# Delta rule's decay matrices: one exponential per head behind a subtraction by VectorE, and the keys' norm factor by a root, multiplied in afterwards

## The chip, the cores and the metric

One core of a Trainium2 chip runs the whole kernel. The metric is the device time of one execution in microseconds, the median of several runs. Times of single instructions come from one profiled execution.

## The reference

One block on 1024 tokens of width 1024, all in float32: a modulated RMS norm, one projection `h @ w_in`, two mixers side by side (dilated attention with 8 heads, and a gated delta rule with 8 heads), `w_out`, then a gated feed-forward and a final norm. The change lies in the delta rule alone. Cut to it:

```python
qkv = silu(causal_conv(concat([q, k, v]), conv_w))      # width 4, per channel
q = l2norm(q) * HEAD_DIM ** -0.5                         # per head of 64
k = l2norm(k)                                            # k * rsqrt(sum(k*k) + EPS)
gcum = cumsum(g)                                         # per chunk and head
diff = gcum[..., :, None] - gcum[..., None, :]
decay = where(causal, exp(where(causal, diff, 0)), 0)
a_mat = where(strict, einsum('cd,ed->ce', k_beta, k) * decay, 0)
sol = triangular_solve(a_mat + I, concat([v * beta, k_beta * exp(gcum)]))
qk = where(causal, einsum('cd,ed->ce', q, k) * decay, 0)
# then a scan over the chunks: v_new, o_i, state
```

## The kernel before

The program runs through these stages: modulation and norm, the projections of `w_in`, the delta rule in two groups `g` of four heads, attention, `w_out`, the feed-forward and the final norm. Each float32 product of the projections is three matmuls over operands split in a high and a low part (names `wh_`, `wl_`, `hh`, `hl`; 512 columns each at L590, 256 at L613). ScalarE makes the high part of a weight, GpSimd the low part (L231).

The delta rule takes chunks of 128 tokens, so a group has 8 chunks `n` for each of its 4 heads. Two heads lie side by side in one tile of 128 partitions. For a group:

1. **Convolutions** (`conv`): ScalarE scales the input into the target, VectorE adds three shifted terms (L553), ScalarE applies SiLU (L557). For group 0 this stands in `delta`, for group 1 in `delta_early`, ahead of the scan of group 0 in time, with a copy to HBM (`cv_d`) that `delta(1)` loads back.
2. **Norms** (`delta_turn`): TensorE transposes keys and queries, ScalarE squares them (L740), VectorE sums them per head (L744): `rk` for keys, `eq` for queries, one number for each token and head (128x32 for a group). Keys are kept transposed in `kt`.
3. **Decay rows** (`delta_rows`): for each head a tile `dt` of 128 x (8 chunks x 128), into which a DMA broadcasts the cumulative decay (`G_d`) of the column's token to all rows; GpSimd's `affine_select` (L712) puts -1e30 where the column's token lies ahead of the row's.
4. **Decay matrices** (`delta_prep`): the keys' factor is made from the sum by a logarithm (L1235 in group 0, L761 in group 1), a product with -0.5 (L762) and an exponential (L763): `rk`. With `lr` = (-0.5 log) - `Gc`, where `Gc` is the row token's own cumulative decay, ScalarE makes `dt` = exp(`dt` + `lr`), one instruction for each head and chunk since the bias is one number for a partition (L767, 8 x 4 for a group). So `dt` holds decay times the row's key factor.
5. **Products** (`delta_prep`): TensorE multiplies keys with queries and with keys (L796, banks `kk_..._q` and `kk_..._k`), and VectorE evicts 16 banks of 512 columns times `dt` (L802) into `qk` and back into `dt`. `nbp`, `nbg`, `kds` are beta, beta times decay, and decay to the chunk's end, each with the keys' factor. The diagonal blocks of `dt` go to HBM (`lt_d`, L809) and come back rearranged as `nt` (L850). GpSimd multiplies `kt` by `kds` (L821) and `qd` by exp of the decay `eb` (L836).
6. **Values** (`delta_v`): convolution, transposes (`trv`, L872), product with beta into `vb` (L875).
7. **Inverse** (`delta_inverse`): `nt` times a factor (L885), then 31 steps of forward substitution on 32x32 blocks by VectorE (L896, L900), a trip through HBM (`tn_d`, L903, `tn`), and then blocks by TensorE for each head (L928 and behind).
8. **Scan** (`delta_scan`): for each chunk TensorE makes the product with the state (`st`, L995), VectorE `R` (L1000), TensorE the new values, ScalarE copies them, TensorE the state's update (L1019); VectorE writes the new state `S`, by a copy for the first chunk (L1028) and with the decay afterwards (L1030).

TensorE is kept busy through these stages by projections of other parts (`g_kd`, `g_qd`, `g_z`, `g_va`, `g_vd`: the projection of keys, queries, gate, attention's values, delta's values) and by the modulations (`mods`, L211). A table (`FILL`) and two functions (`hold`, `until`) say how many microseconds of them stand at each place. The order on each engine and each queue is fixed when the program is built, by a scheduler that weighs estimated durations; `issue_after` forces an instruction behind another. All DMAs stand in one queue, SyncE's, in that order. ScalarE loads a table of functions when it changes between kinds of functions (rows `ACT_TABLE_LOAD`).

Of the kernel before, what the change touches and what calls it, by code (L numbers as in the profile page):

```python
# [12 lines left out]
AF = mybir.ActivationFunctionType  # L13
ALU = mybir.AluOpType
# [4 lines left out]
P = 128  # L19
# [63 lines left out]
def build(tc, I, out):  # L83
    nc = tc.nc
    es = ExitStack()
    op = es.enter_context
# [18 lines left out]
    def urgent():  # L105
# [11 lines left out]
        out=tri, in_=tri, pattern=[[1, P]], compare_op=ALU.is_ge, fill=0.0,  # L117
        base=0, channel_multiplier=-1,
    )
    eps1 = const([P, 1], "eps1")  # L120
# [70 lines left out]
    for j in range(3):  # L191
        n = min(HALF, 1152 - HALF * j)
# [357 lines left out]
    def conv(ci, xp, dst):  # L550
        nc.scalar.activation(dst, xp, AF.Copy, scale=cw[:, ci, 3:4])
        for s_ in range(1, 4):
            nc.vector.scalar_tensor_tensor(  # L553
                out=dst[:, s_:T], in0=xp[:, 0 : T - s_], scalar=cw[:, ci, 3 - s_ : 4 - s_], in1=dst[:, s_:T],
                op0=ALU.mult, op1=ALU.add,
            )
        nc.scalar.activation(dst, dst, AF.Silu)  # L557

    kd, qd = {}, {}
    last, taken = [None], [None]  # L560
# [133 lines left out]
    def bc(v, n):  # L694
        return v.unsqueeze(len(v.shape)).to_broadcast(list(v.shape) + [n])


    sel = {}

    def delta_rows(g):  # L700

        dts = []
        for hl_ in range(4):
            dt_ = pd.tile([P, 8, P], F32, name=f"dt{g}_{hl_}", tag="lu", bufs=5)
            nc.sync.dma_start(
                dt_,
                bass.AP(
                    tensor=_.G.tensor, offset=_.G[0:1, :].offset + (32 * g + hl_) * P,
                    ap=[[0, P], [4 * P, 8], [1, P]],
                ),  # L710
            )
            sel[g] = nc.gpsimd.affine_select(  # L712
                out=dt_, in_=dt_, pattern=[[0, 8], [1, P]], compare_op=ALU.is_ge, fill=-BIG,
                base=0, channel_multiplier=-1,
            )
            dts.append(dt_)
        return dts

    def delta_norms(g):
        n = {}  # L720
        for name in ("rk", "eq", "nbp", "nbg", "kds", "lr"):
            n[name] = pd.tile([P, 8, 4], F32, name=f"{name}{g}", tag=name, bufs=2)
        return n

# [24 lines left out]

    def delta_prep(g, st, norms, kt, lts):  # L750

        rk, eq, nbp, nbg, kds, lr = (norms[k] for k in ("rk", "eq", "nbp", "nbg", "kds", "lr"))
        gs = slice(32 * g, 32 * g + 32)

        def g3(t):
            return t[:, gs].rearrange("p (n h) -> p n h", n=8)

        eqf = eq.rearrange("p n h -> p (n h)")

        if g == 1:  # L760
            nc.scalar.activation(lr, rk, AF.Ln, bias=eps1)  # L761
        nc.vector.tensor_scalar(out=lr, in0=lr, scalar1=-0.5, scalar2=None, op0=ALU.mult)  # L762
        nc.scalar.activation(rk, lr, AF.Exp)  # L763
        nc.vector.tensor_tensor(out=lr, in0=lr, in1=g3(Gc), op=ALU.subtract)
        for h in range(4):
            for n in range(8):
                nc.scalar.activation(lts[h][:, n], lts[h][:, n], AF.Exp, bias=lr[:, n, h : h + 1])  # L767
        nc.vector.tensor_scalar(
            out=eqf, in0=eqf, scalar1=EPS, scalar2=64 * EPS, op0=ALU.add, op1=ALU.mult
        )  # L770
# [12 lines left out]
        for q in range(2):  # L783
            hp = 2 * g + q
# [421 lines left out]
    def fetch(i, name):  # L1206
        xp = pr.tile([P, T], F32, name=f"xp_{name}", tag="xp", bufs=2)
        nc.sync.dma_start(xp, _.pj[i])
        return xp

    def delta_early():

        for j in range(4):
            kind, q = ("k", j) if j < 2 else ("q", j - 2)
            t = pr.tile([P, T], F32, name=f"cv{j}", tag="dt", bufs=2)
            conv((4 if kind == "k" else 0) + 2 + q, fetch(j, f"{kind}{2 + q}"), t)
            delta_turn(1, kind, q, t, norms=norms[1])
            nc.sync.dma_start(_.cv[j], t)

# [3 lines left out]
    def delta(g):  # L1223
        st = {}
        kt = []
        for j in range(4):
            kind, q = ("k", j) if j < 2 else ("q", j - 2)
            hp = 2 * g + q
            t = pd.tile([P, T], F32, name=f"{kind}d{hp}", tag=f"{kind}d", bufs=2)
            (kd if kind == "k" else qd)[hp] = t  # L1230
            if g == 0:
                conv((4 if kind == "k" else 0) + hp, xps[j], t)
                kt.append(delta_turn(g, kind, q, t, norms=norms[0], keep=kind == "k"))
                if j == 1:
                    nc.scalar.activation(norms[0]["lr"], norms[0]["rk"], AF.Ln, bias=eps1)  # L1235
            else:
                nc.sync.dma_start(t, _.cv[j])
                if kind == "k":
                    kt.append(delta_turn(g, kind, q, t, keep=True))
        delta_prep(g, st, norms[g], kt[0:2], delta_rows(g))  # L1240
        rows = delta_rows_in(g, st)
        if g == 1:
            until(lambda: "vd" in done)
        delta_v(g, st, [lambda q=q: vxp[q] if g == 0 else fetch(4 + q, f"v{2 + q}") for q in range(2)], rows)
        delta_inverse(g, st)
        until(lambda: ("z0", "z1")[g] in done)
        delta_scan(g, st)
        if g == 0:
            delta_early()
# [742 lines left out]
```

## Time and profile before

| | |
|---|---|
| median of the runs | 1405.2 us (1401.91 to 1408.69, 3 runs) |
| profiled execution | 1407.41 us |
| its span, first to last instruction | 1405.6 us |
| mean granted TensorE clock | 0.991 |
| decay and products of group 0 | about 120 to 149 us |
| inverse of group 0, first scan | about 172 to 200 us, from 252 us |
| decay and products of group 1 | about 320 to 346 us |

A row of the timeline reads: start and length in us, engine, line, operation, result<-inputs, the engine's partitions x elements, types, count; in brackets the idle time ahead of it and what ended it. A row of the windows reads: window, length, then for TensorE's matmuls, its weight loads, VectorE, ScalarE and GpSimd the busy us and the instructions; then the granted clock, the DMA share and GB/s. Line numbers are those of the kernel before; in rows of the changed kernel the lines behind L712 are higher by 1 to 6.

### The profile page before, as it was taken

To read this page: it belongs to the slowest core of one execution; us is meant where nothing else is said; L and a number is where in the kernel's file an instruction comes from. 1 tells how busy PE (TensorE), PEld (TensorE's weight loads), DVE (VectorE), ACT (ScalarE), POOL (GpSimd) and SP (SyncE) were. 2 spreads that over 40 slices of the span, in tenths; PEclk is the share of its full clock that TensorE was granted. 3 is DMA by queue.
4 is the path that set the end of the run, shared out by engine and by line. 5 is a ranking of instruction groups with operands and counts; after the bars stand their busy time and mean duration, and the time that the engine had idled before them with its cause. 6 is when DMAs were issued, how large, how long until landed. Compare 5 with 4: busy or idle time off the path is not lost.

```text
span 1405.6 us, 24430 instructions
## 1 busy us (share of the span) xinstructions
PE 1353.3 (96%) x8984; PEld 1113.2 (79%) x8984; DVE 874.6 (62%) x1659; ACT 660.0 (47%) x1285; POOL 287.2 (20%) x261
## 2 busy tenths in 40 slices
PE   8998999998999999999999899999999999999997
PEld 4777787888889878777777678888888888888885
DVE  3688573656847242765248987666575776474487
ACT  4497424346233453765168533333333333444456
POOL 2344303324213433543262400000000000000000
PEclk9999999999999999999999999999999999999999
DMA  8666573475362555521675245444453665765566
GB/s 305 225 194 174 173 217 127 135 233 140 120 171 85 173 146 166 158 84 61 198 251 161 97 163 180 157 164 164 137 195 113 209 209 182 255 223 195 195 225 232
DMA packets 169872, 245.65 MB, mean 175 GB/s; under 512 B 32566, under 2 KB 73831, under 8 KB 169752
## 3 DMA queue, kind: packets, MB, share of 16 engines
q1 hardware_dynamic: 169752, 244.08, 54.2%
q8 instruction: 71, 1.16, 0.3%
q14 instruction: 49, 0.40, 0.1%
HBM read 181.27 MB, written 67.48 MB: 177 GB/s over the span
## 4 chain that ended last, share of the span: by engine, by line
PE 71%; DVE 13%; DMA 6%; ACT 4%; issue 3%; POOL 1%; SPq 0%; DVEq 0%; ACTq 0%; POOLq 0%
PE wua L1614 8%; PE wga L1614 8%; PE X L1809 6%; PE g_a L590 4%; PE wuc L1614 4%; PE Z L1809 4%; PE wgc L1614 4%; PE wo L590 3%; PE y L1366 2%; PE Y L1809 2%; PE tr L1349 2%; PE g_va L613 2%; DVE tm L896 2%; PE f L251 2%; PE wgb L1614 2%
## 5 line engine op out<-in xcount | busy, mean ns | idle before, releaser
L1604 DVE TENSOR_TENSOR wl_db<-wr_db,wh_db 128x512 fp32r<-128x512 f32 x77 | 53.2, 690 | 75.7 <-ACT wh_db L1603 75.6
L1603 ACT CAST wh_db<-wr_db 128x512 fp32r<-128x512 f32 x77 | 47.9, 622 | 97.7 <-PE X L1809 41.3
L1329 DVE CUSTOM_DVE_ANT_0 X<-S,ng 128x512 f32<-128x512 f32 (+3 forms) x64 | 36.6, 587 | 61.9 <-PE S L1326 46.4
L1809 PE MATMUL X<-wl_db,wh_da 128*128 128x512 f32 x176 | 68.6, 390 | 0.1
L1336 POOL TENSOR_SCALAR X<-X,sc 128x128 f32<-128x128 f32 (+7 forms) x64 | 50.0, 786 | 91.1 <-DVE sc L1335 77.7
L1809 PE MATMUL X<-wh_db,wl_da 128*128 128x512 f32 x176 | 68.5, 389 | 0.0
L1809 PE MATMUL X<-wh_db,wh_da 128*128 128x512 f32 x176 | 68.5, 389 | 0.0
L1334 ACT ACTIVATE X<-X,sc 128x128 f32<-128x128 f32 (+7 forms) x64 | 49.4, 773 | 33.9 <-DVE sc L1329 31.7
L1604 DVE TENSOR_TENSOR wl_da<-wr_da,wh_da 128x512 fp32r<-128x512 f32 x77 | 52.8, 686 | 1.6 <-ACT wh_da L1603 1.6
L590 PE MATMUL wo<-yh,wh_wo 128*128 128x512 f32 x128 | 51.7, 405 | 1.0 <-DVE xo L1417 1.0
L590 PE MATMUL g_a<-hh,wh_a 128*128 128x512 f32 x128 | 51.8, 404 | 0.0
L590 PE MATMUL wo<-yh,wl_wo 128*128 128x512 f32 x128 | 50.8, 397 | 0.0
L590 PE MATMUL wo<-yl,wh_wo 128*128 128x512 f32 x128 | 50.4, 394 | 0.1
L1603 ACT CAST wh_da<-wr_da 128x512 fp32r<-128x512 f32 x77 | 47.4, 616 | 6.4 <-PE wua L1614 5.9
L590 PE MATMUL g_a<-hl,wh_a 128*128 128x512 f32 x128 | 50.3, 393 | 0.0
L590 PE MATMUL g_a<-hh,wl_a 128*128 128x512 f32 x128 | 50.1, 392 | 0.0
L1603 ACT CAST wh_wg_s<-wg_s 128x512 fp32r<-128x512 f32 x33 | 20.5, 622 | 55.8 <-PE wuc L1614 23.8
L1349 PE MATMUL tr<-ident,X 128*128 128x128 f32 x288 | 42.9, 276 | 1.8 <-ACT et L1354 1.0
L1366 PE MATMUL y<-et,va 128*64 128x128 f32 x576 | 43.9, 280 | 0.0
L231 POOL TENSOR_TENSOR wl_wo<-wr_wo,wh_wo 128x512 fp32r<-128x512 f32 x24 | 32.5, 1357 | 51.7 <-ACT wh_wo L230 51.7
L1603 ACT CAST wh_wg<-wr_wg 128x512 fp32r<-128x512 f32 x31 | 19.3, 621 | 47.2 <-PE wua L1614 19.2
L1603 ACT CAST wh_wu_s<-wu_s 128x512 fp32r<-128x512 f32 x33 | 20.4, 622 | 44.5 <-PE wga L1614 17.5
(545 smaller groups left out, 4349.9 us busy)
## 6 DMA issues: line engine op xcount, KB each, us to landing
wm<-in_wada SPq DMA_DIRECT2D x44, 512.0 KB, 6.0
wr_da<-ao_d SPq DMA_DIRECT2D x77, 256.0 KB, 3.0
wr_wu<-in_wu SPq DMA_DIRECT2D x50, 256.0 KB, 2.8
wr_wg<-in_wg SPq DMA_DIRECT2D x48, 256.0 KB, 3.0
ao_d<-a SPq DMA_DIRECT2D x44, 256.0 KB, 2.6
wr_wd<-in_wdn SPq DMA_DIRECT2D x44, 256.0 KB, 3.0
wr_db<-wt_d SPq DMA_DIRECT2D x44, 256.0 KB, 2.7
ao_d<-as SPq DMA_DIRECT2D x33, 256.0 KB, 2.5
```

The costliest lines, as they stand in the source:

```text
L231: (eng or nc.gpsimd).tensor_tensor(out=lo[:, :n], in0=raw[:, :n], in1=hi[:, :n].bitcast(F32), op=ALU.subtract)
L251: nc.tensor.matmul(first[bank], a[:, w0], b[k][:, cs], start=(k == 0 and n_ == 0), stop=(k == KT - 1 and n_ == 2))
L590: last[0] = nc.tensor.matmul(ps, a[:, w0], b[k0 + k4][:, cs], start=(i == 0), stop=(i == n - 1))
L1329: nc.vector.tensor_tensor_reduce(out=X[:, c0:c1], in0=ps[:, 0 : c1 - c0], in1=ng[:, u + c0 : u + c1], scale=1.0, scalar=(3e38 if m is None ...
L1334: nc.scalar.activation(X[:, 0:nk], X[:, 0:nk], AF.Exp, scale=-1.0, bias=m, accum_out=sc[:, 2:3])
L1336: nc.gpsimd.tensor_scalar(out=X[:, 0:nk], in0=X[:, 0:nk], scalar1=sc[:, 3:4], scalar2=0.0, op0=ALU.mult, op1=ALU.add)
L1349: nc.tensor.transpose(ps[:, (kb - c0) * P : (kb - c0 + 1) * P], X[:, kb * P : kb * P + P], ident)
L1366: nc.tensor.matmul(yps[64 * e : 64 * e + 64, yc], va[:, kb, 64 * e : 64 * e + 64], ets[e][:, kb, :], start=(kb == 0), stop=(kb == qb),)
L1603: nc.scalar.copy(hi, src)
L1604: (eng or nc.vector).tensor_tensor(out=lo, in0=src, in1=hi.bitcast(F32), op=ALU.subtract)
L1614: nc.tensor.matmul(ps, a[:, w0], b, start=(first and k == 0 and n_ == 0), stop=(k == 3 and n_ == 2), skip_group_check=True,)
L1809: nc.tensor.matmul(bank[b], a[:, ts_], w, start=(first and f == 0 and n_ == 0), stop=(f == NF - 1 and n_ == 2), skip_group_check=True,)
```

## The change

For each head VectorE now subtracts the row token's `Gc` from `dt` (128x1024, in `delta_rows`, behind GpSimd's select), and ScalarE takes one exponential of 128x1024 where it took eight of 128x128. The logarithm, the product with -0.5, the exponential of 128x32 and the tile `lr` are gone: `rk` is the square root of the sum plus epsilon (ScalarE, forced behind the last SiLU of the group's convolutions by `issue_after`, with the exponentials forced behind it in the order of heads 3, 0, 1, 2), then a reciprocal by VectorE. VectorE multiplies each `dt` by `rk` afterwards (128x1024 per head). Per group VectorE gets eight operations of 128x1024 and one reciprocal, and loses two of 128x32.

```diff
@@ -554,7 +554,7 @@
                 out=dst[:, s_:T], in0=xp[:, 0 : T - s_], scalar=cw[:, ci, 3 - s_ : 4 - s_], in1=dst[:, s_:T],
                 op0=ALU.mult, op1=ALU.add,
             )
-        nc.scalar.activation(dst, dst, AF.Silu)
+        return nc.scalar.activation(dst, dst, AF.Silu)
 
     kd, qd = {}, {}
     last, taken = [None], [None]
@@ -696,6 +696,7 @@
 
 
     sel = {}
+    silu = [None]
 
     def delta_rows(g):
 
@@ -713,12 +714,16 @@
                 out=dt_, in_=dt_, pattern=[[0, 8], [1, P]], compare_op=ALU.is_ge, fill=-BIG,
                 base=0, channel_multiplier=-1,
             )
+            nc.vector.tensor_tensor(
+                out=dt_, in0=dt_, in1=bc(Gc[:, 32 * g : 32 * g + 32].rearrange("p (n h) -> p n h", n=8)[:, :, hl_], P),
+                op=ALU.subtract,
+            )
             dts.append(dt_)
         return dts
 
     def delta_norms(g):
         n = {}
-        for name in ("rk", "eq", "nbp", "nbg", "kds", "lr"):
+        for name in ("rk", "eq", "nbp", "nbg", "kds"):
             n[name] = pd.tile([P, 8, 4], F32, name=f"{name}{g}", tag=name, bufs=2)
         return n
 
@@ -749,7 +754,7 @@
 
     def delta_prep(g, st, norms, kt, lts):
 
-        rk, eq, nbp, nbg, kds, lr = (norms[k] for k in ("rk", "eq", "nbp", "nbg", "kds", "lr"))
+        rk, eq, nbp, nbg, kds = (norms[k] for k in ("rk", "eq", "nbp", "nbg", "kds"))
         gs = slice(32 * g, 32 * g + 32)
 
         def g3(t):
@@ -757,14 +762,15 @@
 
         eqf = eq.rearrange("p n h -> p (n h)")
 
-        if g == 1:
-            nc.scalar.activation(lr, rk, AF.Ln, bias=eps1)
-        nc.vector.tensor_scalar(out=lr, in0=lr, scalar1=-0.5, scalar2=None, op0=ALU.mult)
-        nc.scalar.activation(rk, lr, AF.Exp)
-        nc.vector.tensor_tensor(out=lr, in0=lr, in1=g3(Gc), op=ALU.subtract)
+        rkf = rk.rearrange("p n h -> p (n h)")
+        with tc.issue_after(silu[0].ins):
+            root = nc.scalar.activation(rkf, rkf, AF.Sqrt, bias=eps1)
+        nc.vector.reciprocal(rkf, rkf)
+        for h in (3, 0, 1, 2):
+            with tc.issue_after(root.ins):
+                root = nc.scalar.activation(lts[h], lts[h], AF.Exp)
         for h in range(4):
-            for n in range(8):
-                nc.scalar.activation(lts[h][:, n], lts[h][:, n], AF.Exp, bias=lr[:, n, h : h + 1])
+            nc.vector.tensor_tensor(out=lts[h], in0=lts[h], in1=bc(rk[:, :, h], P), op=ALU.mult)
         nc.vector.tensor_scalar(
             out=eqf, in0=eqf, scalar1=EPS, scalar2=64 * EPS, op0=ALU.add, op1=ALU.mult
         )
@@ -1213,7 +1219,7 @@
         for j in range(4):
             kind, q = ("k", j) if j < 2 else ("q", j - 2)
             t = pr.tile([P, T], F32, name=f"cv{j}", tag="dt", bufs=2)
-            conv((4 if kind == "k" else 0) + 2 + q, fetch(j, f"{kind}{2 + q}"), t)
+            silu[0] = conv((4 if kind == "k" else 0) + 2 + q, fetch(j, f"{kind}{2 + q}"), t)
             delta_turn(1, kind, q, t, norms=norms[1])
             nc.sync.dma_start(_.cv[j], t)
 
@@ -1229,10 +1235,8 @@
             t = pd.tile([P, T], F32, name=f"{kind}d{hp}", tag=f"{kind}d", bufs=2)
             (kd if kind == "k" else qd)[hp] = t
             if g == 0:
-                conv((4 if kind == "k" else 0) + hp, xps[j], t)
+                silu[0] = conv((4 if kind == "k" else 0) + hp, xps[j], t)
                 kt.append(delta_turn(g, kind, q, t, norms=norms[0], keep=kind == "k"))
-                if j == 1:
-                    nc.scalar.activation(norms[0]["lr"], norms[0]["rk"], AF.Ln, bias=eps1)
             else:
                 nc.sync.dma_start(t, _.cv[j])
                 if kind == "k":
```

The scheduler sets other orders around it. Three places:

**VectorE and SyncE, decay and products of group 0.** In the names `dt_0` to `dt_3` are the four heads' decay tiles, `vd` a value convolution, `kk_0_0_q` a bank of products, `tri` and `mod` belong to the modulations. VectorE before:

```order
L553 SCALAR_TENSOR_TENSOR vd_1759<-xp_v_815,cw,vd_1759 128x1021
L744 TENSOR_REDUCE eq_1373<-sqq_1_1476 128x4x2
L764 TENSOR_TENSOR lr_1377<-lr_1377,Gc 128x32
L771 SCALAR_TENSOR_TENSOR nbp_1374<-beta,rk_1372 128x32
L775 TENSOR_TENSOR kds_1376<-rk_1372,edec 128x32
L774 TENSOR_TENSOR nbg_1375<-nbp_1374,eG 128x32
L744 TENSOR_REDUCE eq_1373<-sqq_0_1518 128x4x2
L779 COPY nbpT_1590<-ps_bp_1588 32x128
L744 TENSOR_REDUCE eq_1373<-sqq_1_1526 128x4x2
L802 TENSOR_TENSOR qk_0_1593<-kk_0_0_q,dt_0_1529 128x512
```

and now, with the four subtractions done further ahead:

```order
L553 SCALAR_TENSOR_TENSOR vd_1735<-xp_v_815,cw,vd_1735 128x1022
L749 TENSOR_REDUCE eq_1373<-sqq_1_1523 128x4x2
L773 TENSOR_TENSOR dt_0_1526<-dt_0_1526,rk_1372 128x1024
L773 TENSOR_TENSOR dt_1_1532<-dt_1_1532,rk_1372 128x1024
L773 TENSOR_TENSOR dt_2_1538<-dt_2_1538,rk_1372 128x1024
L218 STREAM_TRANSPOSE t_1334<-tri 128x128
L773 TENSOR_TENSOR dt_3_1544<-dt_3_1544,rk_1372 128x1024
L222 TENSOR_TENSOR mod<-t_1334,bada 128x4
L774 TENSOR_SCALAR eq_1373<-eq_1373 128x32
L780 TENSOR_TENSOR nbg_1375<-nbp_1374,eG 128x32
L785 COPY nbpT_1566<-ps_bp_1564 32x128
L808 TENSOR_TENSOR qk_0_1569<-kk_0_0_q,dt_0_1526 128x512
```

All four multiplications stand between `kds`, which is just ahead of these rows, and the first eviction, and the last term of the value convolution has moved behind the fourth eviction. On SyncE's queue the load of `nt` stood ahead of the stores of the next projections:

```order
L1132 DMA wm_2_2099<-in_wada 128x2x512
L850 DMA nt_1755<-lt_d 128x1024
L1110 DMA pj_d<-sp_kd_1_0_2003 128x256
L1110 DMA pj_d<-sp_kd_1_1_2006 128x256
L1110 DMA pj_d<-sp_qd_0_0_2066 128x256
L1110 DMA pj_d<-sp_qd_0_1_2069 128x256
```

and now:

```order
L815 DMA lt_d<-dt_3_1544 32x8x32
L1116 DMA pj_d<-sp_kd_1_0_1979 128x256
L1116 DMA pj_d<-sp_kd_1_1_1982 128x256
L1116 DMA pj_d<-sp_qd_0_0_2042 128x256
L1116 DMA pj_d<-sp_qd_0_1_2045 128x256
L856 DMA nt_1731<-lt_d 128x1024
```

It has moved behind four of them. On TensorE, 18 matmuls of `g_kd` and a block of `mods` now stand among the products of this group, which followed each other before; those matmuls stood behind the transposes of the values.

**VectorE, first chunk of the scan of group 0.** `cv` is an early convolution of group 1, `S_1` the state, `dt_0_3512` the first decay tile of group 1. Before:

```order
L553 SCALAR_TENSOR_TENSOR cv_3381<-xp_k_3382,cw,cv_3381 128x1022
L960 TENSOR_TENSOR tc_3_2857<-lw_3_2933,nbp_1374 64x512
L553 SCALAR_TENSOR_TENSOR cv_3381<-xp_k_3382,cw,cv_3381 128x1021
L1028 COPY S_1_1361<-st_0_0_2967 64x64 x2
L1028 COPY S_1_1364<-st_0_1_2968 64x64 x2
L1000 SCALAR_TENSOR_TENSOR R_1_2982<-st_1_0_2983,nbg_1375,vb_1765 128x64 x2
```

and now:

```order
L966 TENSOR_TENSOR tc_3_2833<-lw_3_2909,nbp_1374 64x512
L553 SCALAR_TENSOR_TENSOR cv_3357<-xp_k_3358,cw,cv_3357 128x1021
L717 TENSOR_TENSOR dt_0_3512<-dt_0_3512,Gc 128x1024
L1034 COPY S_1_1361<-st_0_0_2943 64x64 x2
L1034 COPY S_1_1364<-st_0_1_2944 64x64 x2
L1006 SCALAR_TENSOR_TENSOR R_1_2958<-st_1_0_2959,nbg_1375,vb_1741 128x64 x2
```

The first subtraction of group 1 stands ahead of the first copies of the state.

**GpSimd, products of group 1.** `wl_z` and `wl_a` are low parts of weights. Before:

```order
L231 TENSOR_TENSOR wl_z_2_4069<-wr_z_2_4067,wh_z_2_4068 128x512
L821 TENSOR_TENSOR kt_3504<-kt_3504,kds_1382 128x1024
L821 TENSOR_TENSOR kt_3519<-kt_3519,kds_1382 128x1024
L836 TENSOR_TENSOR qd_3532<-qd_3532,eb_3817 128x1024
L836 TENSOR_TENSOR qd_3534<-qd_3534,eb_3823 128x1024
L231 TENSOR_TENSOR wl_z_3_4075<-wr_z_3_4073,wh_z_3_4074 128x512
L231 TENSOR_TENSOR wl_a_0_0_4416<-wr_a_0_0_4414,wh_a_0_0_4415 128x512
```

and now:

```order
L231 TENSOR_TENSOR wl_z_2_4023<-wr_z_2_4021,wh_z_2_4022 128x512
L231 TENSOR_TENSOR wl_z_3_4029<-wr_z_3_4027,wh_z_3_4028 128x512
L231 TENSOR_TENSOR wl_a_0_0_4370<-wr_a_0_0_4368,wh_a_0_0_4369 128x512
L827 TENSOR_TENSOR kt_3480<-kt_3480,kds_1381 128x1024
L827 TENSOR_TENSOR kt_3495<-kt_3495,kds_1381 128x1024
L842 TENSOR_TENSOR qd_3508<-qd_3508,eb_3771 128x1024
L842 TENSOR_TENSOR qd_3510<-qd_3510,eb_3777 128x1024
```

The two weights' low parts have moved ahead of `kt` and `qd`. On TensorE projections of `g_va` and `g_z` stand among this group's products now, and the third value transpose follows them directly.

## The prediction

> **What bounds the kernel now.** I read the share of busy time first, then busy time and clock by stage, then TensorE's waits in the timeline.
>
> ```profile
> PE 1353.3 (96%) x8984; PEld 1113.2 (79%) x8984; DVE 874.6 (62%) x1659; ACT 660.0 (47%) x1285; POOL 287.2 (20%) x261
> ```
>
> TensorE is the bound as a whole. The change adds no TensorE work and takes none, so it can only lengthen or shorten TensorE's waits, or change the clock at which it runs. Both are local, so I look at the stages that the change touches (columns: window, length, then busy us of PE, weight load, DVE, ACT, POOL; then granted clock, DMA share, GB/s).
>
> ```profile
> 130.00:140.00 10.00, 7.28 (x53) 6.21 (x53) 8.83 (x16) 7.80 (x20) 5.67 (x4) 0.89 0.81 202
> 140.00:150.00 10.00, 7.95 (x94) 7.14 (x94) 8.75 (x15) 9.69 (x23) 3.52 (x2) 0.94 0.38 94
> 330.00:340.00 10.00, 7.08 (x75) 6.38 (x72) 9.00 (x11) 7.01 (x12) 7.58 (x3) 0.96 0.27 54
> 340.40:346.00 5.60, 5.59 (x26) 5.59 (x27) 1.03 (x1) 1.33 (x2) 3.23 (x3) 0.50 0.44 115
> 346.00:350.00 4.00, 4.00 (x36) 4.00 (x36) 2.59 (x4) 1.53 (x2) 0.00 (x0) 0.99 0.31 68
> ```
>
> From 130 to 150 us (decay and products of group 0) VectorE is busy 17.6 of 20 us and ScalarE 17.5: both are near their limit, and TensorE waits. The same stage of group 1 runs from about 330 to 346 us. These are TensorE's waits there and behind:
>
> ```profile
> 135.14 0.28 PE L777 MATMUL ps_bp<-ident,nbp 128*32 128x128 f32 x1 [2.01 <-DVE nbp L771]
> 149.77 1.09 PE L872 MATMUL trv<-ident,vd 128*128 128x128 f32 x8 [1.91 <-ACT vd L557]
> 209.03 0.38 PE L613 MATMUL g_z<-wh_z,hh 128*128 128x256 f32 x1 [1.87 <-ACT zt L634]
> 260.41 0.48 PE L995 MATMUL st<-S,kd 128*128 128x128 f32 x2 [1.40 <-DVE S L1030]
> 340.41 0.58 PE L613 MATMUL g_z<-wl_z,hh 128*128 128x256 f32 x1 [3.10 <-POOL wl_z L231]
> ```
>
> They are all that the change can win in these places: some 10 us, and what a low clock costs.
>
> **ScalarE gets shorter.**
>
> ```profile
> 136.88 8.57 ACT L767 ACTIVATE dt<-dt,lr 128x128 f32<-128x128 f32 x29
> 145.36 1.99 ACT L835 ACTIVATE eb<-eb 128x1024 f32<-128x1024 f32 x2
> 131.29 1.28 ACT L763 ACT_TABLE_LOAD   x1
> ```
>
> 29 small exponentials take 8.57 us, 0.295 us each, so 64 take 18.9 us. One of 128x1024 takes 1.0 us by the eb row, so 8 take 8.0: ScalarE loses 11 us, about 5.5 in each group. The logarithm goes and the root comes; by the order of the program there are as many table loads as before (19), at 1.28 us. This gain counts only where ScalarE paces the products; it paces them with VectorE, so what VectorE gets has to be counted first.
>
> **VectorE gets longer.** 16 operations of 128x1024 whose inputs both lie in SBUF.
>
> ```profile
> 352.51 1.22 DVE L885 TENSOR_TENSOR nt<-nt,bpr 128x1024 f32<-128x1024 f32 x1
> 121.75 1.28 DVE L553 SCALAR_TENSOR_TENSOR qd<-xp_f,cw,qd 128x1023 f32<-128x1023 f32 x1 [0.84 <-ACT qd L551]
> 126.36 2.26 POOL L231 TENSOR_TENSOR wl_qd<-wr_qd,wh_qd 128x512 fp32r<-128x512 f32 x1
> 127.39 2.31 DVE L553 SCALAR_TENSOR_TENSOR qd<-xp_f,cw,qd 128x1021 f32<-128x1021 f32 x1
> 135.27 3.78 POOL L821 TENSOR_TENSOR kt<-kt,kds 128x1024 f32<-128x1024 f32 x2 [3.38 <-DVE kds L775]
> 137.62 0.68 DVE L802 TENSOR_TENSOR qk<-kk_q,dt 128x512 f32<-128x512 f32 x1
> 146.57 2.47 DVE L802 TENSOR_TENSOR dt<-kk_k,dt 128x512 f32<-128x512 f32 x4
> L399 DVE RECIPROCAL rr<-rr x1: 1753/1753/1753, 49.5 to 49.5; 128x256 f32<-128x256 f32 x1
> 130.22 0.47 DVE L762 TENSOR_SCALAR lr<-lr 128x32 f32<-128x32 f32 x1
> 134.80 0.18 DVE L764 TENSOR_TENSOR lr<-lr,Gc 128x32 f32<-128x32 f32 x1
> ```
>
> The nt row has the same form: 1.22 us alone, some 0.07 of it under the next, so 1.15 each and 9.2 in a group. Beside a GpSimd operation the convolution takes 2.31 us instead of 1.28, and GpSimd's 2.26: where they meet, one waits for the other. The products' evictions (source in PSUM) keep 0.61 a piece beside GpSimd's kt. The Trainium skill, "SBUF — State Buffer", section "SBUF: two separate sides", calls this pair of ports an exclusive lock, taken by a VectorE operation with two SBUF inputs or by GpSimd, the other blocked for the whole instruction; the trace agrees (2.31 against 1.28), and by it every new operation is exposed where the evictions that they delay are not. Before, kt's 3.78 us ran beside evictions; now, released by kds, they run beside the new multiplications: +3.2, between 0 (no meeting) and 3.8 (all of it). The reciprocal of 32 columns lies between 0.18 us (the subtraction of 128x32) and 1.75 (256 columns); I take 0.4, near the row of its own size, and it cancels with the two lr operations that go (0.47 and 0.18).
>
> Group 0, then: the last eviction ends at 149.04 (146.57 + 2.47), and by the two rows of windows VectorE has 1.2 + 0.2 us idle ahead of that. 9.2 + 3.2 - 1.4 = **11.0 us later**, and TensorE's last product with it: from 147.86 (149.77 less the wait) to 158.9.
>
> ```profile
> 122.04 1.08 PE L211 MATMUL mods<-wm,cc 128*32 128x128 f32 x32
> 124.29 0.39 PE L590 MATMUL g_kd<-hh,wh_kd 128*128 128x512 f32 x1
> 124.52 0.40 PE L590 MATMUL g_kd<-hl,wh_kd 128*128 128x512 f32 x1
> ```
>
> In that time TensorE does 18 projection matmuls (a start each 0.23 us, 4.1) and a block of modulations (1.0) that stood behind the value transposes: 5.1 us. The wait of 1.91 for the value's SiLU goes, for ScalarE is ahead. TensorE: 158.9 - 149.77 - 5.1 = **+4.0** (about +1 if GpSimd never meets the multiplications).
>
> That would be absorbed or not by the next wait, at 209.03. It hangs on the inverse, not on TensorE:
>
> ```profile
> 163.54 0.41 SPq L850 DMA_DIRECT2D nt<-lt_d  x1
> 166.30 0.91 SPq L1110 DMA_DIRECT2D pj_d<-sp_qd  x2
> 171.85 2.27 DVE L885 TENSOR_TENSOR nt<-nt,bpr 128x1024 f32<-128x1024 f32 x1 [12.30 <-DMA nt<-lt_d]
> 202.44 1.15 ACT L551 ACTIVATE cv<-xp_k,cw 128x1024 f32<-128x1024 f32 x1 [4.65 <-DMA tn_d<-tt]
> 207.65 1.06 ACT L557 ACTIVATE cv<-cv 128x1024 f32<-128x1024 f32 x1 [3.78 <-DVE cv L553]
> ```
>
> The inverse's input nt is issued at 163.54 and lands 8.3 us later; at its end ScalarE is held, and zt, for which TensorE waits, stands behind cv. In the new order SyncE issues nt behind the two stores of sp_qd: at 166.30 + 0.91 + 4 = 171.2. With 8.3 us it lands 7.6 us later than before; with 5, since the transfers ahead of it are done by then, 4.3 later. I take **+5.5 us** for group 0; TensorE's own shift (4.0, less the 1.87 that it waits there) is below that.
>
> **Scan of group 0.** Group 1's first subtraction now stands ahead of the first state copies on VectorE, and waits for GpSimd's select of G_d.
>
> ```profile
> 254.16 0.95 DVE L1028 COPY S<-st 64x64 f32<-64x64 f32 x4 [4.33 <-PE st L1019]
> 254.66 1.09 POOL L712 TENSOR_SCALAR_AFFINE_SELECT dt<-dt 128x1024 f32<-128x1024 f32 x1 [3.19 <-DMA dt<-G_d]
> 255.72 1.27 POOL L231 TENSOR_TENSOR wl_va<-wr_va,wh_va 128x512 fp32r<-128x512 f32 x1
> 259.70 1.18 DVE L1030 SCALAR_TENSOR_TENSOR S<-S,eGl,st 64x64 f32<-64x64 f32 x4
> 260.40:264.50 4.10, 4.09 (x19) 3.81 (x20) 2.32 (x9) 0.64 (x2) 1.01 (x1) 0.58 0.15 47
> ```
>
> Queued behind it are S, then R, and the next state's matmul, for which TensorE waits at 260.41. The select ends at 255.75; the subtraction ends at 257 alone and 258.2 behind wl_va, so S goes from 254.16 to 258, of which the slack ahead of S at 259.70 takes back 1.4: **+2.5**, between 0 (the select's load comes earlier) and 4.
>
> **Group 1.** kk is spread among projections and GpSimd does wl_z ahead of kt and qd. So the wait of 3.10 us goes, and the clock of 0.50 behind it: there 26 matmuls took 5.60 us, 0.215 each, and at 0.99 behind that 36 took 4.00, 0.111 each, which makes 26 x 0.104 = 2.7 us. Against this stand the same 9.2 us on VectorE:
>
> ```profile
> 335.83 1.27 DVE L802 TENSOR_TENSOR dt<-kk_k,dt 128x512 f32<-128x512 f32 x2
> 337.03 4.41 DVE L553 SCALAR_TENSOR_TENSOR vd<-xp_v,cw,vd 128x1022 f32<-128x1022 f32 x2
> 338.10 2.25 POOL L231 TENSOR_TENSOR wl_z<-wr_z,wh_z 128x512 fp32r<-128x512 f32 x1
> ```
>
> Three subtractions stand early, beside the convolutions. Four multiplications (4 x 1.15 = 4.6) stand ahead of the evictions, and vd's convolution, which came behind the last of them, is moved ahead too. The last eviction goes from 337.1 to 341.7, but vd was done only at 341.4 (337.03 + 4.41), so the inverse, which needs both, loses nothing by that. TensorE's products end 4.6 us later as well; of these the projections now fill the 2.9 us of gaps that TensorE had from 330 to 340, and 1.7 are given back. 5.8 - 1.7 = **-4.1**, between -5.8 (nothing given back) and 0 (the gaps are not filled, and the low clock comes ahead of the products instead).
>
> Sum: 5.5 + 2.5 - 4.1 = **+3.9 us**. The profiled execution took 1407.4 us, so 1411.3; its span is 1405.6. It lies 2.2 above the median of the runs, 1405.2, from which I count: 1405.2 + 3.9 = 1409.
>
> **Rivals.** *A, not slower:* the wait at wl_z and its clock go whole (-5.8), the selects land early enough that the scan loses nothing, and nt lands with TensorE's own shift (4.0 - 1.87 = +2.1). It holds if wl_z is ready when TensorE comes to it. Sum -3.7: 1401.5; with the waits at 135.14 and 149.77 gone as well (-3.9), 1397.6. For it: 340.4 is the largest loss here. Against: it needs GpSimd, VectorE and SyncE to fall well. 0.20.
> *B, slower by more:* the subtraction ahead of the state copies costs its 4, nt its 7.6, and in group 1 TensorE waits ahead of the products what it waited at wl_z (0): +11.6: 1417. It decides when TensorE's new gaps pass 3 us, for 3.10 us was followed by a clock of 0.50. By the Trainium skill, "TensorE: Matmul & The Clock Gate", section "Part 1: The HAM clock gate", the array drops to half clock after about 3.4 us idle; here 1.40 us of wait was followed by 0.58 already, so shorter waits count too. 0.27.
> *C, the change does not do what it says:* with 19 table loads and the evictions as they were, ScalarE's 11 us were never on the path, and VectorE's come under TensorE's fill: 1405, 1403 to 1407. 0.13.
>
> **How the numbers follow.** My sum 0.40, between 1405 and 1413. Half a per cent, 7 us, is about what a measurement of this kernel tells from no change (its runs spread over 6.8): faster is below 1398.2, slower above 1412.2. A gives 0.10 faster, 0.10 same; C same; my sum 0.27 same, 0.13 slower; B 0.03 same, 0.24 slower: 0.10, 0.53, 0.37. The range goes from A's middle to a little above B: 1400 to 1420.
>
> **What would show it.** ScalarE's busy sum down 11 us, VectorE's up 18 or more; the last eviction of group 0 near 160 and of group 1 near 342; nt of group 0 landing at 176 to 180; the first S copy at 258; no wait for wl_z at 340 and a clock near 1 behind it. I am wrong if nt lands before 174, if the new VectorE operations are far from 1.15 us, or if kt does not hold the multiplications.

## The result

The changed kernel takes 1414.87 us (median of 6 runs, 1414.52 to 1416.0), the kernel before 1405.35 beside it (6 runs). The ratio is 1.0065 with a 95% interval from 1.0049 to 1.0081: slower by 9.1 us, between 7 and 11. It lies in the range of 1400 to 1420, but above the forecast of 1409 and above the 1405 to 1413 of the prediction's own sum, nearer to rival B (1417). The profiled execution took 1414.53 us, its span is 1412.8, 7.2 above that of before. Below, microseconds of a measurement are the ratio less 1 times 1405; those of a trace come from one execution, and both are told apart.

The share of busy time of the changed kernel, first line of its page:

```profile
PE 1356.2 (96%) x8984; PEld 1115.3 (79%) x8984; DVE 900.4 (64%) x1673; ACT 649.0 (46%) x1227; POOL 293.0 (21%) x261
```

ScalarE is 11.0 us shorter (660.0 before), VectorE 25.8 longer (874.6), where the prediction had 18 or more. TensorE is the bound as before. The windows of the two stages (window, length, busy us of PE, weight load, DVE, ACT, POOL, clock, DMA share, GB/s):

```profile
130.00:140.00 10.00, 7.92 (x71) 5.99 (x73) 10.00 (x11) 7.84 (x11) 6.67 (x4) 1.00 0.63 159
140.00:150.00 10.00, 6.43 (x50) 5.27 (x42) 9.63 (x13) 4.22 (x6) 5.02 (x3) 0.81 0.70 199
330.00:340.00 10.00, 7.62 (x46) 6.58 (x44) 9.89 (x12) 6.11 (x7) 4.68 (x3) 0.70 0.71 173
340.00:350.00 10.00, 9.85 (x97) 9.25 (x97) 6.58 (x12) 3.67 (x4) 4.58 (x2) 0.79 0.17 28
```

ScalarE, which was busy 17.5 of 20 us in group 0, has 8 us free there now, and VectorE, which was busy 17.6, has 0.4: where two engines were near their limit, VectorE alone is left as the bound of the stage. In group 1 the low clock of 340 to 346 has not gone, it has moved ahead. TensorE's waits, those that answer to the ones of before:

```profile
136.84 0.28 PE L783 MATMUL ps_bp<-ident,nbp 128*32 128x128 f32 x1 [2.08 <-DVE nbp L777]
147.64 1.43 PE L802 MATMUL kk_q<-qd,kd 64*128 64x128 f32 x5 [3.57 <-DVE nbpT L785]
167.77 1.09 PE L878 MATMUL trv<-ident,vd 128*128 128x128 f32 x8 [0.81 <-ACT vd L557]
213.20 0.38 PE L613 MATMUL g_z<-wh_z,hh 128*128 128x256 f32 x1 [0.91 <-ACT zt L634]
261.55 0.46 PE L1001 MATMUL st<-S,kd 128*128 128x128 f32 x2 [3.67 <-DVE S L1034]
333.06 1.22 PE L802 MATMUL kk_q<-qd,kd 64*128 64x128 f32 x8 [2.38 <-DVE nbpT L785]
365.77 0.38 PE L613 MATMUL g_z<-wh_z,hh 128*128 128x256 f32 x1 [2.33 <-ACT zt L634]
```

The wait of 3.10 for wl_z and the 1.91 for the first value's SiLU are gone (0.81 is left, at the second value). In their place stand 3.67 at the state's matmul, 2.38 among group 1's products and 2.33 behind them, and in group 0 one of 3.57 at 147.64, for nbpT.

The new operations, as the list of groups has them (busy us, mean ns of one, idle before):

```profile
L773 DVE TENSOR_TENSOR dt<-dt,rk 128x1024 f32<-128x1024 f32 x8 | 14.3, 1814 | 0.0
L717 DVE TENSOR_TENSOR dt<-dt,Gc 128x1024 f32<-128x1024 f32 x8 | 13.0, 1654 | 7.6 <-POOL dt L713 7.6
```

16 operations take 27.3 us. At the 1.22 us that one takes alone it would be 19.5.

### The profile page after: what moved, and what is told of

The parts are those of the page before. It is cut to its first block, busy times and chain, and to the rows that moved or that the text cites. A ratio compares the mean times of both kernels' runs of the same rounds, so it can differ in the third digit from the quotient of the medians.

```text
span 1412.8 us, 24378 instructions
## 1 busy us (share of the span) xinstructions
PE 1356.2 (96%) x8984; PEld 1115.3 (79%) x8984; DVE 900.4 (64%) x1673; ACT 649.0 (46%) x1227; POOL 293.0 (21%) x261
## 4 chain that ended last, share of the span: by engine, by line
PE 74%; DVE 15%; DMA 5%; issue 3%; ACT 2%; POOL 1%; SPq 0%; DVEq 0%; ACTq 0%; POOLq 0%
PE wga L1618 8%; PE wua L1618 8%; PE X L1813 6%; PE g_a L590 5%; PE wo L590 4%; PE wuc L1618 4%; PE wgc L1618 4%; PE Z L1813 4%; PE y L1370 2%; PE Y L1813 2%; PE tr L1353 2%; DVE tt L906 2%; PE f L251 2%; PE wgb L1618 2%; PE wub L1618 2%
## 5 line engine op out<-in xcount | busy, mean ns | idle before, releaser
L1353 PEld LDWEIGHTS tr<-ident,X 128*128 128x128 f32 x288 | 33.2, 140 | 10.1 <-issue 5.7
```

Source lines behind the costliest of these rows:

```text
L1353: nc.tensor.transpose(ps[:, (kb - c0) * P : (kb - c0 + 1) * P], X[:, kb * P : kb * P + P], ident)
```

## The experiments

The theory after the traces: ScalarE's shorter time is a real gain; VectorE's new operations cost more than that, in three places: in front of the evictions of both groups, and in front of the first state copies; and they are long where GpSimd works beside them. The rivals: ScalarE's time never counted; the bank that ps_bp holds is the price, not VectorE's time; the loss is spread over the program. The changed kernel was measured once, beside 6 runs of the kernel before; kernels of different rounds are compared by their ratios to the kernel before in the same round, whose median lay between 1405.35 and 1409.99. The diffs are shortened, and show each kernel against the changed one.

**One group at a time.** Both kernels keep the code of before for the other group.

```diff
+            if g == 0:   # in the second kernel: if g == 1
+                nc.vector.tensor_tensor(out=dt_, in0=dt_, in1=bc(Gc...), op=ALU.subtract)
...
+        if g == 0:
+            (root, reciprocal, one exponential a head, multiplications)
+        else:
+            (logarithm, lr, 32 exponentials with a bias)
```

> The change in group 0 alone; group 1 keeps the logarithm, the bias and the 32 small exponentials. If the loss is the sum of three places (group 0's decay and products, the scan of group 0 behind group 1's first subtraction, group 1's products), only the first stays: between +2.5 and +4 us to the kernel before, 1408 to 1409.5, the first copy of S without a subtraction ahead of it, and group 1's products as before with the wait for wl_z. Rival, the loss hangs on the number of operations in general (tables, semaphores, VectorE's share): half of it, +4.7, whatever the place. Rival, group 0's loss is absorbed by later waits and all of it comes from group 1: 0 to +1.

> The change in group 1 alone; group 0 as before. Sum of three places: the scan's (2.3 us by the trace) and group 1's (2.6 us) stay: +4.5 to +6.5, 1410 to 1412. If half of the loss comes from each group: +4.7, not told apart from that. If group 1 carries nearly all: +8 to +9.5. The state's first copy behind the subtraction as in the changed kernel, TensorE's wait for nbpT among the products and the low clock behind it as there.

Group 0 alone: 1.0015 (0.9992 to 1.0038), +2 us. Group 1 alone: 1.0047 (1.0024 to 1.0070), +6.6 us. Their sum, 8.7, is the changed kernel's 9.1, so the two groups account for it, and most comes from group 1's code. In the first kernel the first copies of the state start without a subtraction ahead of them and TensorE waits for wl_z as before:

```profile
256.83 0.95 DVE L1045 COPY S<-st 64x64 f32<-64x64 f32 x4 [4.33 <-PE st L1036]
341.78 0.58 PE L613 MATMUL g_z<-wl_z,hh 128*128 128x256 f32 x1 [3.08 <-POOL wl_z L231]
```

In the second, the state's wait and the wait for nbpT are there, with a clock of 0.50 behind the latter:

```profile
257.64 0.76 PE L1012 MATMUL st<-S,kd 128*128 128x128 f32 x2 [3.57 <-DVE S L1045]
329.43 0.79 PE L813 MATMUL kk_q<-qd,kd 64*128 64x128 f32 x2 [2.39 <-DVE nbpT L796]
330.00:335.00 5.00, 5.00 (x31) 4.55 (x30) 4.90 (x5) 2.48 (x3) 1.04 (x1) 0.50 0.60 154
335.00:340.00 5.00, 5.00 (x29) 4.55 (x29) 2.65 (x5) 1.37 (x2) 0.00 (x0) 0.56 0.20 41
```

**The subtraction ahead of the state copies.** Group 1's subtractions are forced behind the last state update of group 0. On VectorE's list that moves the first of them and nothing else of weight.

```diff
+            with tc.issue_after(copied[0].ins) if g else ExitStack():
                 nc.vector.tensor_tensor(out=dt_, in0=dt_, in1=bc(Gc...), op=ALU.subtract)
...
-                            nc.vector.scalar_tensor_tensor(out=Sn[q]...
+                            copied[0] = nc.vector.scalar_tensor_tensor(out=Sn[q]...
```

> The changed kernel with group 1's subtractions forced behind the last update of group 0's state; on VectorE that moves one operation, the first subtraction, and nothing else of weight. If it holds the state's chain as the trace says (S copied at 260.95 instead of about 256.9): 2.3 to 4 us less than the changed kernel, 1411 to 1412.6, and TensorE's wait of 3.67 at the second state matmul gone or below 1. Rival, the chain of the scan has slack later on (the early convolutions of group 1, the readout): 1414 to 1415.

1.0033 (1.0012 to 1.0053), +4.6 us, so some 4.5 below the changed kernel, though the two intervals just touch. The place in the changed kernel (VectorE and GpSimd):

```profile
257.54 1.09 POOL L713 TENSOR_SCALAR_AFFINE_SELECT dt<-dt 128x1024 f32<-128x1024 f32 x1 [3.36 <-DMA dt<-G_d]
258.60 1.26 POOL L231 TENSOR_TENSOR wl_va<-wr_va,wh_va 128x512 fp32r<-128x512 f32 x1
258.66 2.27 DVE L717 TENSOR_TENSOR dt<-dt,Gc 128x1024 f32<-128x1024 f32 x1 [6.13 <-POOL dt L713]
260.95 0.95 DVE L1034 COPY S<-st 64x64 f32<-64x64 f32 x4
```

and with the subtractions late:

```profile
258.76 0.95 DVE L1036 COPY S<-st 64x64 f32<-64x64 f32 x4 [4.33 <-PE st L1027]
265.00 0.46 PE L1003 MATMUL st<-S,kd 128*128 128x128 f32 x2 [1.39 <-DVE S L1038]
```

VectorE stood 6.13 us for the select, then the subtraction took 2.27 us beside wl_va, and the copies only then. Without it the copies wait for TensorE's st alone, as before, and the wait of 3.67 is gone; the wait of 1.39 is that of before (1.40).

**kt behind the multiplications.** kds, which releases GpSimd's kt, is put behind the fourth multiplication.

```diff
-        nc.vector.tensor_tensor(out=kds, in0=rk, in1=g3(edec), op=ALU.mult)
+        with tc.issue_after(rooted.ins):        # rooted: the last dt *= rk
+            nc.vector.tensor_tensor(out=kds, in0=rk, in1=g3(edec), op=ALU.mult)
```

> The changed kernel with kds, and by it GpSimd's kt times kds, behind the four multiplications of dt in each group. If the lock between GpSimd and VectorE lengthens them (four took 8.4 us in group 0, 4.6 would be their time alone), the last eviction of group 0 ends 3 to 4 us earlier, at 156.5 to 157.5, group 1's by 1 to 2, and the time falls by 3 to 5: 1410 to 1412. Rival, kt meets other operations of VectorE instead and holds as much there, or the evictions are not what the inverse waits for: 1414 to 1415.5.

1.0039 (1.0016 to 1.0063), +5.5 us: alone not told apart from the changed kernel. The changed kernel in group 0, kt and three of the multiplications:

```profile
136.97 5.75 POOL L827 TENSOR_TENSOR kt<-kt,kds 128x1024 f32<-128x1024 f32 x2 [3.33 <-DVE kds L781]
138.60 6.33 DVE L773 TENSOR_TENSOR dt<-dt,rk 128x1024 f32<-128x1024 f32 x3
```

and with the edit, two of them and the fourth:

```profile
138.20 2.35 DVE L773 TENSOR_TENSOR dt<-dt,rk 128x1024 f32<-128x1024 f32 x2
143.49 1.18 DVE L773 TENSOR_TENSOR dt<-dt,rk 128x1024 f32<-128x1024 f32 x1
148.56 2.65 DVE L553 SCALAR_TENSOR_TENSOR vd<-xp_v,cw,vd 128x1021 f32<-128x1021 f32 x1
157.04 2.48 DVE L809 TENSOR_TENSOR dt<-kk_k,dt 128x512 f32<-128x512 f32 x4 [0.42 <-PE kk_k L803]
```

6.33 for three became 1.2 a piece, so kt did hold them. But the last eviction ends at 159.5, only 0.9 earlier: the value's convolution is held as before (2.65, and 2.87 in the changed kernel), and the evictions wait for TensorE. In group 0 kt's hold was real and its removal was worth little. In group 1 the edit does less than its name says. There the multiplication to which kds is tied, the fourth in the program, is the first that VectorE does, so kt still runs beside the other three, the last two of which take 5.00:

```profile
333.52 5.89 POOL L828 TENSOR_TENSOR kt<-kt,kds 128x1024 f32<-128x1024 f32 x2 [0.28 <-DVE kds L782]
335.49 5.00 DVE L773 TENSOR_TENSOR dt<-dt,rk 128x1024 f32<-128x1024 f32 x2
```

**Both edits.**

> The changed kernel with group 1's subtractions behind the last state update and kds behind the multiplications: the two edits tried singly (0.33% and 0.39% above the kernel before, where the changed kernel is at 0.65%). If each removes a cost of its own: 0 to +0.2% to the kernel before, 1405 to 1408.5. If kds' edit gained nothing and its run was chance: +0.3%, as the late subtractions alone. Faster than the kernel before only if both were undervalued.

0.9990 (0.9969 to 1.0010): no difference from the kernel before, and clearly below the changed kernel. The two edits, which change no arithmetic and no count, take away the whole loss; no gain is left either. The place can be followed by the first state copies of each group, which stood at 254.16 and 420.49 in the kernel before and stand at 260.95 and 427.70 in the changed kernel:

```profile
256.50 0.95 DVE L1037 COPY S<-st 64x64 f32<-64x64 f32 x4 [4.33 <-PE st L1028]
422.40 0.46 DVE L1037 COPY S<-st 64x64 f32<-64x64 f32 x2 [3.84 <-PE st L1028]
```

Of 7.2 us at group 1's scan 1.9 are left. By which way the second edit helps in group 1, where kt still runs beside three multiplications, the runs don't show. There kds and nbpT, the copy that TensorE waited for, now stand ahead of those three, and that wait is gone.

**The bank of ps_bp.** ScalarE copies nbpT instead of VectorE.

```diff
-        nc.vector.tensor_copy(nbpT, ps[:32, 0:P])
+        nc.scalar.copy(nbpT, ps[:32, 0:P])
```

> The changed kernel with the copy of ps_bp into nbpT made by ScalarE instead of VectorE, so that its bank comes free without waiting behind the multiplications; else the same order. If TensorE's waits of 3.57 and 2.38 us are the price of that bank: they go, the clock stays near 1 behind 333, and the time falls by 3 to 6, to 1409 to 1412. If the multiplications in front of the evictions are the cause and the bank only the place where it shows: the wait moves to the next bank, 1414 to 1415.5.

1.0086 (1.0060 to 1.0112), +12.1 us, above both expectations. The waits moved to the next bank, which VectorE had to evict, and grew in group 1:

```profile
150.69 3.74 PE L802 MATMUL kk_k<-kd 64*128 64x128 f32 x30 [2.49 <-DVE qk L808]
342.12 1.43 PE L802 MATMUL kk_q<-qd,kd 64*128 64x128 f32 x5 [3.61 <-DVE qk L808]
```

So freeing that bank wins nothing: TensorE then waits for VectorE's next eviction, behind the same multiplications. By its interval this kernel is not told apart from the changed one, and surely no gain.

**Halves of the change, and GpSimd in VectorE's place.** Subtractions alone (the factor by logarithm in the bias), multiplications alone (-Gc as bias), and the whole change with the subtractions by GpSimd.

```diff
+                for n in range(8):      # subtractions alone; lr = -0.5 log(sum)
+                    nc.scalar.activation(lts[h][:, n], lts[h][:, n], AF.Exp, bias=lr[:, n, h : h + 1])
...
+                for n in range(8):      # multiplications alone; lr = -Gc
+                    root = nc.scalar.activation(lts[h][:, n], lts[h][:, n], AF.Exp, bias=lr[:, n, h : h + 1])
...
-            nc.vector.tensor_tensor(out=dt_, ..., op=ALU.subtract)
+            sel[g] = nc.gpsimd.tensor_tensor(out=dt_, ..., op=ALU.subtract)
```

> Half of the change: VectorE subtracts Gc from dt (four of 128x1024 a group), but the keys' factor stays in the bias of the 32 small exponentials, by logarithm as before; no multiplications. If the loss of the changed kernel (0.65%, 9 us) is VectorE's added time where it stands in front of the evictions and of the state copies: the scan's part (about 4.5 us by the run with late subtractions) stays, the rest falls by half, +5 to +6. If the multiplications alone make the loss in the two product stages: +4 to +5. If the subtractions make all of it: +8 to +9.

> The other half: 32 small exponentials a group with -Gc as bias, so that they wait for no norm, root and reciprocal as in the changed kernel, and VectorE's four multiplications; no subtractions, nothing ahead of the state copies. Sum of places: the scan's part gone, multiplications in front of the evictions: +3 to +5. If ScalarE's time counts as well, which is that of the kernel before here: +5 to +7. If subtractions make all of the loss: 0 to +1.

> The changed kernel with GpSimd in VectorE's place for the eight subtractions, each behind its select. If VectorE's busy time and its order are what counts: the state copies stand free, group 0's evictions end 4 to 6 us earlier, +1 to +4 to the kernel before. If the shared ports count (GpSimd at 1.9 us an operation holds VectorE's convolutions as long): no better than the changed kernel less the scan's part, +4 to +6; the convolutions beside it at 2.3 us instead of 1.28 then.

All three missed, upwards: 1.0106 (1.0078 to 1.0134), 1.0075 (1.0053 to 1.0097) and 1.0130 (1.0102 to 1.0157). Each half alone costs as much as the whole or more. That a half has VectorE's time without ScalarE's gain does not explain it, for all of VectorE's operations without ScalarE's gain cost 12.6 us (below). The scheduler gave each kernel an order of its own, so the halves don't add up and I read no sum from them. With subtractions alone a wait of 2.60 at 136.51 is followed by more than 16 us at half clock:

```profile
137.00:153.00 16.00, 16.00 (x79) 14.68 (x81) 9.88 (x15) 10.54 (x36) 4.39 (x2) 0.50 0.50 123
```

With GpSimd in VectorE's place the two engines hold each other: its subtraction takes 1.91 us at the shortest and 2.76 in the median, and VectorE's convolutions beside it (2.33 for one) and multiplications beside kt (8.54 for three) are long as well.

```profile
126.53 2.77 POOL L717 TENSOR_TENSOR dt<-dt,Gc 128x1024 f32<-128x1024 f32 x1
128.04 2.33 DVE L553 SCALAR_TENSOR_TENSOR qd<-xp_f,cw,qd 128x1021 f32<-128x1021 f32 x1
142.27 8.54 DVE L773 TENSOR_TENSOR dt<-dt,rk 128x1024 f32<-128x1024 f32 x3
```

Multiplications alone lose most of their 10.5 us behind the products. Group 1's nt is multiplied at 354.33, 1.8 us later than before, and its first state copies start at 431.11, 10.6 later. Between them lies a stretch of the inverse that the kernel before does at full clock (first row) and this one at half clock (second):

```profile
396.00:413.00 17.00, 16.84 (x386) 14.56 (x386) 9.63 (x23) 6.54 (x17) 3.17 (x4) 1.00 0.29 83
400.00:417.00 17.00, 17.00 (x211) 14.91 (x201) 6.20 (x14) 4.01 (x11) 2.21 (x3) 0.50 0.22 71
```

Why the clock falls there is not settled; waits of 1.73 and 1.31 us stand ahead of it.

**The two sides of the change apart.** ScalarE's short exponentials without VectorE's operations, and VectorE's operations with ScalarE's 64 pieces. The first kernel leaves out the row token's decay and the keys' factor, so it does not compute the reference.

```diff
-            nc.vector.tensor_tensor(out=lts[h], in0=lts[h], in1=bc(rk[:, :, h], P), op=ALU.mult)
-                root = nc.scalar.activation(lts[h], lts[h], AF.Exp)
+                root = nc.scalar.activation(lts[h], lts[h], AF.Exp, bias=low4)   # and no subtraction
...
-                root = nc.scalar.activation(lts[h], lts[h], AF.Exp)
+                for n in range(8):      # the second kernel
+                    root = nc.scalar.activation(lts[h][:, n], lts[h][:, n], AF.Exp)
```

> ScalarE's side of the change alone: one exponential of 128x1024 a head (with a constant bias of -4 that keeps the numbers in range), root and reciprocal; VectorE's subtractions and multiplications are left out, so dt holds neither the row token's decay nor the keys' factor. If ScalarE's 11 us were a bound beside VectorE, as the profile of before says (17.5 busy of 20 us), this is faster than the kernel before by 3 to 9 us. If ScalarE was never on the path: -1 to +1.

> The changed kernel with its exponentials in pieces of 128x128 again (32 a group, no bias), so VectorE has all its new work and ScalarE the time of before; it computes the same. Together with the run of ScalarE's side alone this makes the square of both sides. If the sides add: this is above the changed kernel by what ScalarE's side alone gains, +12 to +18 to the kernel before. If ScalarE has slack once VectorE is longer: as the changed kernel, +8 to +10.

ScalarE's side alone: 0.9954 (0.9937 to 0.9972), 6.5 us faster than the kernel before. VectorE's side alone: 1.0090 (1.0061 to 1.0120), 12.6 slower. So the gain that the change is after is there, and ScalarE was on the path. Beside VectorE's work it counts less: from 12.6 to 9.1 it is 3.5, with intervals that overlap, so that it counts at all there is not shown. In group 0 of the first kernel the evictions start at 136.0 and end at 146.65 (before 137.62 and 149.04):

```profile
136.00 2.48 DVE L804 TENSOR_TENSOR qk<-kk_q,dt 128x512 f32<-128x512 f32 x4
144.18 2.47 DVE L804 TENSOR_TENSOR dt<-kk_k,dt 128x512 f32<-128x512 f32 x4
```

**One operation instead of two.** lr is made as before and added to dt; then one exponential a head.

```diff
-            (subtraction in delta_rows, root, reciprocal, multiplication)
+            nc.vector.tensor_tensor(out=lts[h], in0=lts[h], in1=bc(lr[:, :, h], P), op=ALU.add)
+            nc.scalar.activation(lts[h], lts[h], AF.Exp)
```

> One exponential a head with one operation of VectorE instead of two: lr = -0.5 log(sum) - Gc is made as before and added to dt (128x1024), so root, reciprocal and multiplications go and the 9.2 us a group of added VectorE time become 4.6; the additions wait for the norms. If VectorE's added time is the price: between the changed kernel and before, +1 to +5. If what counts is that VectorE's work now stands between norms and first exponential, in front of all evictions: +6 to +10.

1.0005 (0.9982 to 1.0027): no difference from the kernel before, below both expectations. Half of VectorE's added time with the same gain of ScalarE comes out even. That would fit a price of VectorE's time, but the halves above, which add eight operations of 128x1024 as well, cost 14.9 and 10.5. They keep ScalarE's long side, which was worth 3.5 to 6.5, and that does not make up the difference; so time alone doesn't set the loss. Its last evictions end between those of before and of the changed kernel (156.2 and 342.7). No kernel of this study that computes the reference is faster than the one before.

## Why the prediction came out as it did

The forecast was +3.9 and +9.1 was measured. The kind was right, slower and by less than one per cent, and the range holds it. But the time lies above the 1412.2 from which the prediction calls a kernel slower, to which it gave 0.37, and not in the stretch to which it gave 0.53.

**ScalarE, 11 us less, on the path beside VectorE:** right (649.0 against 660.0), and the run of its side alone shows 6.5 us as time. Rival C, that it never counted, fell.

**VectorE's operations at 1.15 us, and 3.2 a group 0 for kt:** too low, and by the prediction's own sign (far from 1.15 us) wrong. They take 1.65 and 1.81 us in the mean. Beside kt, which was foreseen, they meet the selects and the weights' low parts. Two rows of group 0:

```profile
128.78 5.94 DVE L717 TENSOR_TENSOR dt<-dt,Gc 128x1024 f32<-128x1024 f32 x3
157.93 2.47 DVE L808 TENSOR_TENSOR dt<-kk_k,dt 128x512 f32<-128x512 f32 x4
```

Three subtractions take 5.94 us. Still the last eviction ends at 160.4, where 160 was foreseen. That is luck: group 0's eight operations take about 15.6 us where 12.4 were counted, and the last six convolution terms ahead of the last eviction take 9.6 where they took 11.3; the rest is not traced.

**nt and TensorE's wait behind the inverse, +5.5:** the way was right, the size a little high.

```profile
172.28 0.41 SPq L856 DMA_DIRECT2D nt<-lt_d  x1
176.20 1.23 DVE L891 TENSOR_TENSOR nt<-nt,bpr 128x1024 f32<-128x1024 f32 x1 [6.44 <-DMA nt<-lt_d]
```

Issued at 172.28 (171.2 foreseen), it landed 3.9 us later instead of 5 to 8.3, at the lower end of 176 to 180; the wait moved from 209.03 to 213.20, +4.2. By the first copies of the state in the kernel with group 0 alone (256.83 against 254.16) 2.7 of it are left, and the measurement of that kernel says 2 (-1 to 5).

**Scan, +2.5, between 0 and 4:** right in its mechanism. The copies start 4.1 us behind those of the kernel with group 0 alone; TensorE's wait there is 3.67 against 1.40, 2.3 more. Measured by the late subtractions it is about 4.5.

**Group 1, -4.1: the step that failed.** The wait for wl_z went, as foreseen. That the projections fill the gaps, that only 1.7 us are given back and that the clock stays near 1 did not hold. On VectorE and GpSimd:

```profile
327.41 2.33 DVE L773 TENSOR_TENSOR dt<-dt,rk 128x1024 f32<-128x1024 f32 x1
330.84 3.84 POOL L827 TENSOR_TENSOR kt<-kt,kds 128x1024 f32<-128x1024 f32 x2
330.93 1.89 DVE L774 TENSOR_SCALAR eq<-eq 128x32 f32<-128x32 f32 x1
332.73 0.27 DVE L785 COPY nbpT<-ps_bp 32x128 f32<-32x128 f32 x1
344.26 1.29 DVE L808 TENSOR_TENSOR dt<-kk_k,dt 128x512 f32<-128x512 f32 x2 [2.98 <-PE kk_k L802]
348.99 2.48 DVE L808 TENSOR_TENSOR dt<-kk_k,dt 128x512 f32<-128x512 f32 x4
```

kt holds even a 128x32 operation for 1.89 us (0.17 in group 0, at 147.13), nbpT stands behind it, and TensorE comes to a stop for 2.38 us at 333.06. Then its clock falls:

```profile
335.00:340.00 5.00, 5.00 (x30) 4.60 (x30) 4.89 (x6) 1.13 (x2) 0.00 (x0) 0.50 0.76 181
340.00:345.00 5.00, 5.00 (x32) 4.78 (x32) 2.02 (x5) 3.32 (x4) 0.53 (x1) 0.57 0.01 1
```

For ten microseconds (334.0 to 344.2) TensorE is full and at half speed, so the products come late and VectorE waits for them (2.98 at 344.26). The last eviction ends at 351.5. The forecast was 341.7, which becomes 346.7 with the 5.0 us that group 0 and its scan brought along; it came 4.8 us later than that. The inverse starts 7.0 us later than before (355.70 and 362.69), 2.0 more than it was behind already, where 4.1 less was foreseen. This is what rival B said of group 1: TensorE waits ahead of the products what it waited at wl_z, and the low clock with it. B's price for that was 0, and 2 it was; its other two terms (4 and 7.6) were too high.

The sum by the trace: 2.7 (group 0) + 2.3 (scan) + 2.2 (group 1 and what is behind) = 7.2, the difference of the spans. The first is read from the kernel with group 0 alone, and the last is what remains. The largest chance went to a sum in which one stage pays back; none did. That the clock fell because of the wait is read from its place and not shown: no run kept TensorE busy over that wait, and the last section has waits of the same size at full clock.

## What to carry to other kernels

Work moved from one engine to another is priced at the rate that the receiving engine has in that stage, beside the work that it meets there (here 1.65 and 1.81 us instead of 1.22), and by its busy share there and not in the whole: VectorE was at 17.6 of 20 us. Then look at the order that the new instructions get: here two forced orders, a 128x1024 subtraction behind a recurrence instead of ahead of it and a later release of a GpSimd product, took back the whole loss. When a gain does not show, measure its side alone: 6.5 us were there.

## What the runs showed that was not expected

A wait of 2.38 us of TensorE was followed by ten microseconds at a clock of 0.50, one of 2.39 by the same in the kernel with group 1 alone; before, 3.10 were followed by 5.6 us at 0.50. So the clock can cost more than the wait ahead of it. But it need not fall: the changed kernel waits 2.33 us at 365.77, and the kernel with ScalarE's side alone 2.36 at 326.32, and behind both it stays at 1.00 (in this order):

```profile
364.00:372.00 8.00, 6.23 (x52) 6.23 (x53) 7.31 (x21) 1.24 (x4) 0.00 (x0) 1.00 0.39 128
328.00:336.00 8.00, 7.32 (x68) 6.94 (x67) 6.03 (x9) 3.40 (x5) 6.30 (x3) 1.00 0.19 30
```

So the length of the wait does not decide it. In windows of half a microsecond the stretches at half clock last 3.4 us or 2, 3 or 5 times as long: four of 3.4 and one of 6.8 in the kernel before, three of 3.4, one of 6.8 and one of 10.2 in the changed one, between 100 and 1400 us. That is 20.4 and 27.2 us in all. At half speed 3.4 us lose 1.7, so by this estimate up to 3.4 us of the 7.2 between the two traces come through the clock. Runs of one kernel differ in it too: beside the last runs the kernel before took 1402.32 us at a mean clock of 0.993 and 1416.81 at 0.984. A term of 2 us that is read from one trace is no larger than one such stretch. The Trainium skill, "TensorE: Matmul & The Clock Gate", section "Part 1: The HAM clock gate", gives about 3.4 us of idle time as what brings the array to half clock; these waits are shorter, with and without a fall of the clock, and the measurements decide.

A VectorE operation of 128x32 with one input in SBUF was held for 1.89 us by GpSimd's kt, like those with two inputs. The Trainium skill, "SBUF — State Buffer", section "SBUF: two separate sides", has the same lock for operations in a mode that uses two ports; whether this one ran in such a mode the trace doesn't show.
